# Row sums of the adaLN projection: a fixed place behind TensorE's order, a load per short step

## The chip, the core and the metric

The kernel runs on one NeuronCore of a Trainium2 chip. The metric is the time of one execution on the device in microseconds (us). Before the change, three runs gave 1697.73, 1699.33 and 1700.04 us, a median of 1699.33 us. An execution under the profiler took 1700.17 us, and its trace spans 1698.4 us.

The engines are TensorE (PE; PEld is its weight load), VectorE (DVE), ScalarE (ACT), GpSimd (POOL) and SyncE (SP), which here only issues DMA transfers, one after the other in one queue.

## What is computed

Two layers of a backbone block on 256 context tokens and 256 latent tokens of width 2048. Cut to what matters:

```python
def _layer(x, ctx, c, c_ctx, ...):
    shift, scale, gate = jnp.split(jax.nn.silu(c) @ w_ada + b_ada, 3, axis=-1)
    shift_c, scale_c, gate_c = jnp.split(jax.nn.silu(c_ctx) @ w_ada + b_ada, 3, axis=-1)
    h = _rms_norm(x, norm_w) * (1.0 + scale[:, None]) + shift[:, None]
    hc = _rms_norm(ctx, norm_w) * (1.0 + scale_c) + shift_c
    p = jnp.split(h @ w_in, offsets, axis=-1)       # and pc from hc
    ...                                             # four head groups: attention, LRU, DeltaNet, latent attention
    x = x + gate[:, None] * (jnp.concatenate([y_a, y_b, y_c, y_d], axis=-1) @ w_out)
    ...                                             # the same for ctx in the first layer
```

`w_ada` is 2048 x 6144 for each layer, and it is multiplied by two vectors only (the conditioning of the latent and of the context tokens). That product is what the change is about.

## The kernel before

**Projections.** Activations lie feature by token, 512 tokens wide. Each weight is split into a high and a low part (`hi`, `lo`), and a 128 x 128 block costs three matmuls. Weights come in units of 128 x 512: a load `raw` on SP's queue (3 buffers), `hi` by ScalarE, `lo = raw - hi` by VectorE (3 buffers each), then 12 matmuls into a `gm` buffer. `lo` is VectorE's part of every unit, so a late VectorE makes TensorE wait after at most the units that are already split. The last stage of each layer, the output projection, reads such units from `w_out` with `yhi` and `ylo` on the other side, and VectorE adds each result to the residual `xo`.

**adaLN by row sums.** Chunks 0 to 7 of layer 0 are computed on TensorE at the start (`ada_pe`). All others, 8 to 11 of layer 0, 0 to 7 of layer 1 (both during layer 0), and 8 to 11 of layer 1 (during layer 1), go through `ada_bg`: a chunk is 16 transfers of 128 x 512 from a transposed `w_ada` into `araw`, which has 2 buffers. For each, VectorE runs a SCALAR_TENSOR_TENSOR that multiplies by the conditioning vector `crow` and sums the rows into a column of `acc` (`aacc`). With two vectors it runs twice: the first writes its product to `junk`, the last over `araw` itself. The latent-only chunks of layer 1 need it once. That makes 192 loads with two row sums and 64 with one, 448 row sums. After a chunk, `ada_sum` folds `acc` by four small matmuls and adds the bias. A load can go out when the last row sum on its buffer is done.

**What sets the order.** Tasks are Python generators that a model clock (`Flow`) interleaves: each issued matmul moves the clock, and a task that yields a number sleeps so long. TensorE's instructions are pinned in the order in which they are issued (`in_order`); the weight loads are pinned among themselves (`load`, "load order"). All others are placed by a list scheduler with priorities, which simulates the engines and gives each a fixed order; on the chip an engine works through its own order and waits where an operand isn't there. `self.behind(i, name, why)` adds an edge that only the order sees: `i` may stand no earlier than `name`. It makes no wait on the chip.

In `ada_bg` before, each step issues a load and, at once, its row sums, at a lowered priority (`high_priority(-100)`); then it sleeps `self.pace` (2.8 in layer 0's projections, 4.0 in layer 1's, 2.0 in the output projections), and longer while the model of VectorE is over 1.0 us behind. Only each eighth load has an edge to the last weight load. The scheduler so puts the row sums where its own simulation has the transfer landed and VectorE free. `Flow` wakes tasks between groups of three matmuls, so steps come out in multiples of a group.

Of the kernel before, what the change touches and what calls it, by code (L numbers as in the profile page):

```python
# [191 lines left out]
class Block:  # L192
# [300 lines left out]
    def ada_bg(self, items):  # L493


        if not hasattr(self, "crow"):
            self.ada_rows()
        for l, ch in items:
            nv = 2 if l == 0 or ch < 8 else 1
            acc = self.st([128, nv, 16], "aacc")  # L500
            for j in range(16):
                raw = self.st([128, 512], "araw")
                i = self.nc.sync.dma_start(out=raw, in_=self.io["w_ada"][12 * l + ch - 8, j])
                if j % 8 == 0:
                    self.behind(i.ins, self.last_load, "load order")
                with self.tc.high_priority(-100):
                    for v in range(nv):
                        self.dve.scalar_tensor_tensor(
                            out=raw if v == nv - 1 else self.junk, in0=raw, scalar=1.0, in1=self.crow[:, v, :],
                            op0=ALU.mult, op1=ALU.mult, accum_out=acc[:, v, j:j + 1])  # L510
                yield self.pace
                while self.dve.behind() > self.LIM:
                    yield self.dve.behind() - self.LIM + 0.1
            self.flow.spawn(self.ada_sum(l, ch, acc), self.dve.behind() + self.rest)

    def ada_sum(self, l, ch, acc):
        p = self.pt([128, 4, acc.shape[1]])
# [966 lines left out]
    def layer(self, l):  # L1484
        nc, flow = self.nc, self.flow
        self.l = l
        self.qt = [0, 1, 2, 3] if l < LAYERS - 1 else [2, 3]
        self.t0 = 0 if l < LAYERS - 1 else TC
        self.yd = self.tc.dram_tile([12, 128, T], F32, name=f"yd{l}")
        self.hs, self.y, self.cq, self.cv = [], {}, {}, {}  # L1490
        self.vq = self.one([128, 4, 4], "vq")
        flow.done = {e for e in flow.done if e.startswith("ada")}
        flow.spawn(self.start0() if l == 0 else self.start1())
        pss = yield from (self.gemm_pairs if l == 0 else self.gemm_multi)(self.FIRST[l])
        if l == 0:
            self.pace, self.rest = 2.8, 14.0
            flow.spawn(self.ada_bg([(0, ch) for ch in range(8, 12)] + [(1, e) for e in range(8)]))
        else:
            self.pace, self.rest = 4.0, 14.0
            flow.spawn(self.ada_bg([(1, ch) for ch in range(8, 12)]))  # L1500
        flow.spawn(self.krab(pss[0]))
        if l == 0:
            flow.spawn(self.ak_tile(0, pss[5]))
        flow.spawn(self.c_keys(pss[1:5]))
        flow.spawn(self.c_scan())
        flow.spawn(self.d_split())
        flow.spawn(self.attend(self.a_chains()))
        flow.spawn(self.attend(self.d_chains()))
        todo = {"ak": self.ak_tile, "av": self.av_tile, "aq": self.aq_tile, "cq": self.cq_tile, "cv": self.cv_tile,
                "dkv": self.dkv_tile, "dq": self.dq_tile, "bx": self.bx_tile, "zb": self.zb_tile}  # L1510
        for name in self.ORDER[l]:
            if name in self.AFTER and (l == 0 or name != "dkv0"):
                yield self.AFTER[name]
            g, i = name[:-1], int(name[-1])
            if g == "up":
                yield from self.d_up(i)
                continue
            ps = yield from self.gemm(self.t0 if g in ("cq", "dq", "aq") or g[0] == "z" else 0)
            flow.spawn(todo[g](i, ps) if g in todo else self.z_tile(g[1], i, ps))
        yield "d3"  # L1520
        self.pace, self.rest = 2.0, 8.0
        if l == LAYERS - 1:
            self.rawtag, self.nraw = "r2", 5
        yield from self.out_proj(l)
# [137 lines left out]
```

## Time and profile before

| | before |
|---|---|
| median of three runs | 1699.33 us |
| the profiled execution | 1700.17 us, span 1698.4 us |
| TensorE busy | 1612.3 us (95%) |
| VectorE busy | 1210.3 us (71%) |
| ScalarE, GpSimd busy | 723.4 us (43%), 266.8 us (16%) |
| granted TensorE clock, mean | 0.986 |

Busy shares are means over stages that differ. TensorE's idle time is 86.1 us of the span. The row sums are the two SCALAR_TENSOR_TENSOR groups on `crow`; the numbers behind the bar in a group's row are its busy time, the mean of one in ns, and the time in which the engine stood idle before it, with what ended most of that wait. A wait of an engine in its own order also holds all that stands behind the waiting instruction.

### The profile page before, as it was taken

The page shows a single profiled execution, that of the slowest core. Times are in us where ns is not written, and L with a number is a line of the kernel's source. Part 1 is how long each engine was busy: PE and PEld are TensorE (multiplying, and loading weights), DVE is VectorE, ACT ScalarE, POOL GpSimd, SP SyncE. Part 2 cuts the span into 40 slices and gives each one's busy share as a digit, 9 for nine tenths or more (in the row PEclk, how much of TensorE's full clock was granted, in tenths as well). Part 3 has the DMA queues.
Part 4 walks back from the last instruction along what each step waited for, and adds up shares of the span by engine and source line. Part 5 has one row for each costly group of instructions (what it writes and reads, how often), then busy time and mean ns, then how long its engine had stood idle before and what let it go on. Part 6 is the DMA issues. An engine that isn't in the chain of part 4 may idle for free.

```text
span 1698.4 us, 27629 instructions
## 1 busy us (share of the span) xinstructions
PE 1612.3 (95%) x9888; PEld 1310.2 (77%) x9888; DVE 1210.3 (71%) x2852; ACT 723.4 (43%) x1365; POOL 266.8 (16%) x351
## 2 busy tenths in 40 slices
PE   3999999899999999999999998999899999999999
PEld 2666777678888877667877776778788989677899
DVE  4336877698888768787977758665766777565854
ACT  4224342243333344476522235445442324656843
POOL 0000327513032000000011100031842012100000
PEclk8999999999999999999999999999999999999999
DMA  8995435533523645435677645444554524433575
GB/s 311 333 345 178 143 109 147 149 117 112 159 79 95 204 144 159 134 114 172 198 226 228 209 137 155 139 132 121 169 176 129 174 88 141 118 100 105 180 231 155
DMA packets 145657, 276.61 MB, mean 163 GB/s; under 512 B 16620, under 2 KB 25712, under 8 KB 145520
## 3 DMA queue, kind: packets, MB, share of 16 engines
q1 hardware_dynamic: 143328, 269.81, 51.4%
q0 software_dynamic: 1328, 4.33, 1.1%
q8 instruction: 78, 1.28, 0.3%
q10 hardware_dynamic: 864, 0.71, 0.1%
q14 instruction: 59, 0.48, 0.1%
HBM read 261.81 MB, written 13.11 MB: 162 GB/s over the span
## 4 chain that ended last, share of the span: by engine, by line
PE 67%; DMA 12%; DVE 8%; POOL 6%; issue 6%; ACT 1%; SPq 0%; ACTq 0%; DVEq 0%; POOLq 0%
PE gm L231 42%; PE px L231 22%; DMA araw<-w_ada 9%; POOL Xs L184 3%; PE px L236 3%; POOL ct L184 2%; DVE lo L184 2%; DVE junk L184 1%; DMA ls<-C 1%; DVE araw L184 1%; DMA xk<-xT 1%; ACT hi L184 1%; DMA raw<-w_first 1%; DMA Ls<-ls 1%; DVE xo L184 0%
## 5 line engine op out<-in xcount | busy, mean ns | idle before, releaser
L231 PE MATMUL gm<-hhi,hi 128*128 128x512 f32 (+1 forms) x1296 | 497.3, 384 | 2.9 <-ACT hi L184 2.6
L184 ACT ACTIVATE hi<-raw 128x512 fp32r<-128x512 f32 (+1 forms) x454 | 282.2, 626 | 495.2 <-PE gm L231 334.8
L184 DVE TENSOR_TENSOR lo<-raw,hi 128x512 fp32r<-128x512 f32 (+1 forms) x454 | 325.6, 719 | 219.7 <-ACT hi L184 210.4
L231 PE MATMUL gm<-hhi,lo 128*128 128x512 f32 (+1 forms) x1296 | 463.6, 358 | 5.9 <-DVE lo L184 5.8
L231 PE MATMUL gm<-hlo,hi 128*128 128x512 f32 (+1 forms) x1296 | 461.1, 356 | 0.0
L231 PEld LDWEIGHTS gm<-hhi,hi 128*128 128x128 f32 x1296 | 246.3, 190 | 56.1 <-issue 24.5
L231 PEld LDWEIGHTS gm<-hhi,lo 128*128 128x128 f32 x1296 | 245.6, 190 | 44.9 <-DVE lo L184 8.2
L231 PEld LDWEIGHTS gm<-hlo,hi 128*128 128x128 f32 x1296 | 246.8, 190 | 32.7 <-issue 5.3
L184 DVE SCALAR_TENSOR_TENSOR araw<-araw,crow 128x512 f32<-128x512 f32 x256 | 185.1, 725 | 22.4 <-DMA araw<-w_ada 19.3
L184 DVE SCALAR_TENSOR_TENSOR junk<-araw,crow 128x512 bf16<-128x512 f32 x192 | 138.1, 719 | 48.9 <-DMA araw<-w_ada 48.3
L231 PE MATMUL gm<-yhi,lo 128*128 128x512 f32 (+1 forms) x416 | 141.8, 341 | 6.0 <-DVE lo L184 5.8
L231 PE MATMUL gm<-yhi,hi 128*128 128x512 f32 (+1 forms) x416 | 140.4, 337 | 0.0
L231 PE MATMUL gm<-ylo,hi 128*128 128x512 f32 (+1 forms) x416 | 140.0, 336 | 0.0
L231 PEld LDWEIGHTS gm<-yhi,lo 128*128 128x128 f32 x416 | 78.9, 190 | 20.8 <-DVE lo L184 13.0
L231 PEld LDWEIGHTS gm<-ylo,hi 128*128 128x128 f32 x416 | 79.0, 190 | 8.3
L231 PEld LDWEIGHTS gm<-yhi,hi 128*128 128x128 f32 x416 | 79.0, 190 | 7.5
L231 PE MATMUL px<-hhi,hi 128*128 128x512 f32 x176 | 75.0, 426 | 8.7 <-ACT hhi L184 7.7
L231 PE MATMUL px<-hlo,hi 128*128 128x512 f32 x176 | 71.9, 408 | 0.2 <-DVE hlo L184 0.2
L231 PE MATMUL px<-hhi,lo 128*128 128x512 f32 x176 | 71.1, 404 | 0.0
L231 PE MATMUL gm<-araw,csil 128*32 128x128 f32 x1024 | 38.5, 290 | 29.2 <-DMA araw<-w_ada 28.7
L184 DVE TENSOR_TENSOR lo<-r,hi 128x512 fp32r<-128x512 f32 x62 | 42.9, 692 | 32.7 <-ACT hi L184 30.8
L184 POOL TENSOR_TENSOR sqa<-sqa,sqx 128x512 f32<-128x512 f32 x12 | 17.9, 1494 | 278.1 <-ACT sqx L184 278.1
(326 smaller groups left out, 2505.3 us busy)
## 6 DMA issues: line engine op xcount, KB each, us to landing
raw<-w_in SPq DMA_DIRECT2D x344, 256.0 KB, 2.7
araw<-w_ada SPq DMA_DIRECT2D x256, 256.0 KB, 2.9
araw<-w_ada SPq DMA_DIRECT2D x64, 512.0 KB, 5.6
raw<-w_out SPq DMA_DIRECT2D x66, 256.0 KB, 2.8
r<-w_out SPq DMA_DIRECT2D x62, 256.0 KB, 3.3
raw<-w_first SPq DMA_DIRECT2D x24, 256.0 KB, 6.6
xk<-xT SPq DMA_DIRECT2D x16, 256.0 KB, 5.2
xo<-xT SPq DMA_DIRECT2D x16, 256.0 KB, 3.9
```

Of the source, the lines that this page charges most:

```text
L184: return getattr(self.eng, name)(*a, **kw)
L231: self.in_order(self.nc.tensor.matmul(out, lhsT=lhsT, rhs=rhs, start=start, stop=stop), us or max(n, 128) * passes / 2400.0)
L236: self.in_order(self.nc.tensor.transpose(out, in_, self.c["ident"][b:b + n, b:b + n]), 0.107)
```

## The change

A step now issues the load of row-sum item n, sleeps half a pace, issues the row sums of item n-1, and sleeps the other half. The row sums so are issued one and a half steps behind their load. Every load has an edge to the last weight load and one to the last issued matmul, and each row sum has an edge to the last matmul issued. `ada_sum` is started directly behind the last row sums of a chunk. The pace in layer 0's projections goes from 2.8 to 2.2; 4.0 and 2.0 stay. The number of instructions of each kind on each engine is unchanged.

```diff
-            acc = self.st([128, nv, 16], "aacc")
-            for j in range(16):
+        todo, raws, acc = [(l, ch, j) for l, ch in items for j in range(16)], [], None
+        for n in range(len(todo) + 1):
+            if n < len(todo):
+                l, ch, j = todo[n]
                 raw = self.st([128, 512], "araw")
                 i = self.nc.sync.dma_start(out=raw, in_=self.io["w_ada"][12 * l + ch - 8, j])
-                if j % 8 == 0:
-                    self.behind(i.ins, self.last_load, "load order")
+                self.behind(i.ins, self.last_load, "load order")
+                self.behind(i.ins, self.last_pe, "paced")
+                raws.append(raw)
+            yield 0.5 * self.pace
+            if n:
+                l, ch, j = todo[n - 1]
...
+                while self.dve.behind() > self.LIM:
+                    yield self.dve.behind() - self.LIM + 0.1
+                raw = raws.pop(0)
                 with self.tc.high_priority(-100):
                     for v in range(nv):
-                        self.dve.scalar_tensor_tensor(
+                        i = self.dve.scalar_tensor_tensor(
...
+                        self.behind(i.ins, self.last_pe, "paced")
+                if j == 15:
+                    self.flow.spawn(self.ada_sum(l, ch, acc), self.dve.behind() + self.rest)
+            yield 0.5 * self.pace
...
-            self.pace, self.rest = 2.8, 14.0
+            self.pace, self.rest = 2.2, 14.0
```

VectorE in layer 0's output projection. Before, where `lo_8471` and the next two `lo` stand (numbers tell buffers apart; `araw_8531` and `araw_8562` are two loads):

```order
L184 TENSOR_TENSOR lo_8471<-raw_8468,hi_8470 128x512
L184 SCALAR_TENSOR_TENSOR junk_1487,aacc_8530<-araw_8531,crow_1485 128x512
L184 TENSOR_TENSOR lo_8493<-raw_8490,hi_8492 128x512
L184 SCALAR_TENSOR_TENSOR araw_8531,aacc_8530<-araw_8531,crow_1485 128x512
L184 SCALAR_TENSOR_TENSOR junk_1487,aacc_8530<-araw_8562,crow_1485 128x512
L184 SCALAR_TENSOR_TENSOR araw_8562,aacc_8530<-araw_8562,crow_1485 128x512
L184 TENSOR_TENSOR lo_8515<-raw_8512,hi_8514 128x512
L184 SCALAR_TENSOR_TENSOR junk_1487,aacc_8530<-araw_8584,crow_1485 128x512
```

The same place of the projection now (`lo_8531` and the two after it; `araw_8495`, `araw_8526` and `araw_8548` are three loads):

```order
L184 TENSOR_TENSOR lo_8531<-raw_8528,hi_8530 128x512
L184 SCALAR_TENSOR_TENSOR junk_1487,aacc_8267<-araw_8495,crow_1485 128x512
L184 SCALAR_TENSOR_TENSOR araw_8495,aacc_8267<-araw_8495,crow_1485 128x512
L184 TENSOR_TENSOR lo_8553<-raw_8550,hi_8552 128x512
L184 SCALAR_TENSOR_TENSOR junk_1487,aacc_8267<-araw_8526,crow_1485 128x512
L184 SCALAR_TENSOR_TENSOR araw_8526,aacc_8267<-araw_8526,crow_1485 128x512
L184 TENSOR_TENSOR lo_8575<-raw_8572,hi_8574 128x512
L184 SCALAR_TENSOR_TENSOR junk_1487,aacc_8267<-araw_8548,crow_1485 128x512
```

The two row sums of a load now stand together, one pair behind each `lo`; before, a `lo` stood between them in one unit and two pairs followed each other in another.

SP's queue at that place, before:

```order
L503 DMA araw_8531<-w_ada 128x512
L503 DMA araw_8562<-w_ada 128x512
L265 DMA raw_8544<-w_out 128x512
L1544 DMA xo_9138<-xT 128x512
L645 DMA xk_9593<-x1d_8068 128x512
L265 DMA raw_8566<-w_out 128x512
L503 DMA araw_8584<-w_ada 128x512
L503 DMA araw_8606<-w_ada 128x512
```

And now:

```order
L503 DMA araw_8526<-w_ada 128x512
L265 DMA raw_8603<-w_out 128x512
L503 DMA araw_8548<-w_ada 128x512
L1554 DMA xo_9173<-xT 128x512
L265 DMA raw_8625<-w_out 128x512
L655 DMA xk_9593<-x1d_8129 128x512
L503 DMA araw_8570<-w_ada 128x512
L265 DMA raw_8647<-w_out 128x512
```

Loads of `araw` went out in pairs with a weight load behind them; now one stands between two weight loads.

VectorE in layer 1, at an attention head (`mx` and `P` belong to its softmax), before:

```order
L184 TENSOR_TENSOR lo_11437<-raw_11434,hi_11436 128x512
L184 SCALAR_TENSOR_TENSOR ya1_11443<-zt_11444,gm_11322 128x256
L184 TENSOR_REDUCE mx_11449<-px_11447 128x1
L184 SCALAR_TENSOR_TENSOR araw_11556,aacc_11417<-araw_11556,crow_1485 128x512
L184 TENSOR_TENSOR lo_11471<-raw_11468,hi_11470 128x512
L184 SCALAR_TENSOR_TENSOR mx_11449<-mx_11449,a_rs_10337 128x1
L184 SCALAR_TENSOR_TENSOR araw_11626,aacc_11417<-araw_11626,crow_1485 128x512
L184 RECIPROCAL mx_11449<-mx_11449 128x1
L184 TENSOR_SCALAR P_11452<-P_11452,mx_11449 128x512
L184 TENSOR_TENSOR lo_11505<-raw_11502,hi_11504 128x512
```

And now:

```order
L184 TENSOR_TENSOR lo_11423<-raw_11420,hi_11422 128x512
L184 SCALAR_TENSOR_TENSOR ya1_11429<-zt_11430,gm_11312 128x256
L184 TENSOR_REDUCE mx_11437<-px_11435 128x1
L184 SCALAR_TENSOR_TENSOR mx_11437<-mx_11437,a_rs_10333 128x1
L184 SCALAR_TENSOR_TENSOR araw_11332,aacc_10274<-araw_11332,crow_1485 128x512
L184 TENSOR_TENSOR lo_11459<-raw_11456,hi_11458 128x512
L184 RECIPROCAL mx_11437<-mx_11437 128x1
L184 TENSOR_SCALAR P_11440<-P_11440,mx_11437 128x512
L184 TENSOR_TENSOR lo_11491<-raw_11488,hi_11490 128x512
```

Row sums stood between two `lo` each time; now one stands where two stood, and its load went out well before the weight loads of these units.

## Rows read from the trace of the kernel before

**Rows 1.** The page: span, and busy time of the engines.
```profile
span 1698.4 us, 27629 instructions
PE 1612.3 (95%) x9888; PEld 1310.2 (77%) x9888; DVE 1210.3 (71%) x2852; ACT 723.4 (43%) x1365; POOL 266.8 (16%) x351
```

**Rows 2.** The page's groups of row sums: busy, mean ns, idle before, releaser.
```profile
L184 DVE SCALAR_TENSOR_TENSOR araw<-araw,crow 128x512 f32<-128x512 f32 x256 | 185.1, 725 | 22.4 <-DMA araw<-w_ada 19.3
L184 DVE SCALAR_TENSOR_TENSOR junk<-araw,crow 128x512 bf16<-128x512 f32 x192 | 138.1, 719 | 48.9 <-DMA araw<-w_ada 48.3
```

**Rows 3.** Waits of TensorE: total us, times, longest.
```profile
PE gm L231 <- DVE lo L184: 11.6, 15, 2.7
```

**Rows 4.** Busy by stretch: length, engines, clock, DMA share, GB/s.
```profile
255.00:849.00 594.00, 578.48 (x3027) 458.83 (x3026) 475.88 (x1173) 254.16 (x473) 106.84 (x132) 0.99 0.48 142
789.00:849.00 60.00, 60.00 (x265) 48.04 (x264) 54.19 (x115) 38.76 (x59) 0.00 (x0) 1.00 0.68 204
886.00:986.00 100.00, 94.42 (x410) 72.56 (x408) 78.68 (x187) 25.18 (x43) 13.22 (x9) 1.00 0.71 216
```

**Rows 5.** Chain of waits from 870 to 1000: start, us, what.
```profile
886.34 4.01 DMA araw<-w_ada
...
891.68 0.62 DVE araw L184 x2
...
892.32 3.59 DMA araw<-w_ada
...
898.65 3.17 DMA araw<-w_ada
```

**Rows 6.** The same stretches for instructions on gm, then on px.
```profile
886.00:986.00 100.00, 94.21 (x394) 72.25 (x392) 7.49 (x16) 0.00 (x0) 1.00 0.71 216
...
886.00:986.00 100.00, 0.50 (x16) 0.31 (x16) 0.53 (x4) 0.00 (x0) 1.00 0.71 216
```

**Rows 7.** Chain of waits, 535 to 564: matmuls in a row.
```profile
535.50 27.25 PE gm L231 x120
```

**Rows 8.** DMA issues from 860 to 1000; then of the whole span.
```profile
araw<-w_ada SPq DMA_DIRECT2D x39, 256.0 KB, 3.6
...
araw<-w_ada SPq DMA_DIRECT2D x256, 256.0 KB, 2.9
```

**Rows 9.** Timeline of VectorE: row sums that waited, idle time in brackets.
```profile
229.54 0.69 DVE L184 SCALAR_TENSOR_TENSOR junk<-araw,crow 128x512 bf16<-128x512 f32 x1 [1.96 <-DMA araw<-w_ada]
...
326.51 0.69 DVE L184 SCALAR_TENSOR_TENSOR junk<-araw,crow 128x512 bf16<-128x512 f32 x1 [3.37 <-DMA araw<-w_ada]
...
1204.66 1.01 DVE L184 SCALAR_TENSOR_TENSOR araw<-araw,crow 128x512 f32<-128x512 f32 x1 [1.43 <-DMA araw<-w_ada]
...
1240.69 0.69 DVE L184 SCALAR_TENSOR_TENSOR araw<-araw,crow 128x512 f32<-128x512 f32 x1 [0.99 <-DMA araw<-w_ada]
...
1245.13 0.69 DVE L184 SCALAR_TENSOR_TENSOR araw<-araw,crow 128x512 f32<-128x512 f32 x1 [0.86 <-DMA araw<-w_ada]
```

**Rows 10.** Timeline of TensorE: matmuls that waited.
```profile
239.15 0.42 PE L236 MATMUL px<-cst,P 128*128 128x128 f32 x2 [2.53 <-DVE P L184]
...
327.95 0.63 PE L231 MATMUL gm<-hhi,lo 128*128 128x512 f32 x1 [2.73 <-DVE lo L184]
...
1206.71 0.38 PE L231 MATMUL gm<-hhi,lo 128*128 128x256 f32 x1 [2.07 <-DVE lo L184]
...
1248.31 0.66 PE L236 MATMUL px<-cst,P 128*128 128x128 f32 x4 [3.19 <-DVE P L184]
```

**Rows 11.** Timelines of GpSimd and ScalarE around a chain on GpSimd.
```profile
288.13 0.94 POOL L184 TENSOR_TENSOR ct<-Ls,Xs 128x238 f32<-128x238 f32 x1
...
293.89 0.62 POOL L184 TENSOR_TENSOR ct<-Ls,Xs 128x238 f32<-128x238 f32 x1
...
314.17 0.21 ACT L184 ACTIVATE gw<-rowp 128x8 f32<-128x8 f32 x1 [8.14 <-POOL Xs L184]
```

**Rows 12.** Waits of SP's queue, 860 to 1000: total us, times, longest.
```profile
SPq L503 <- DVE araw L184: 24.2, 28, 1.9
```

More of the change, by code (lines that the diff above doesn't have):

```diff
@@ L497, in ada_bg @@
             self.ada_rows()
-        for l, ch in items:
-            nv = 2 if l == 0 or ch < 8 else 1
-            acc = self.st([128, nv, 16], "aacc")
-            for j in range(16):
+        todo, raws, acc = [(l, ch, j) for l, ch in items for j in range(16)], [], None
+        for n in range(len(todo) + 1):
+            if n < len(todo):
+                l, ch, j = todo[n]
                 raw = self.st([128, 512], "araw")
                 i = self.nc.sync.dma_start(out=raw, in_=self.io["w_ada"][12 * l + ch - 8, j])
-                if j % 8 == 0:
-                    self.behind(i.ins, self.last_load, "load order")
+                self.behind(i.ins, self.last_load, "load order")
[4 more added lines that the diff above has]
+                l, ch, j = todo[n - 1]
+                nv = 2 if l == 0 or ch < 8 else 1
+                if j == 0:
+                    acc = self.st([128, nv, 16], "aacc")
+                while self.dve.behind() > self.LIM:
+                    yield self.dve.behind() - self.LIM + 0.1
+                raw = raws.pop(0)
                 with self.tc.high_priority(-100):
                     for v in range(nv):
-                        self.dve.scalar_tensor_tensor(
+                        i = self.dve.scalar_tensor_tensor(
                             out=raw if v == nv - 1 else self.junk, in0=raw, scalar=1.0, in1=self.crow[:, v, :],
                             op0=ALU.mult, op1=ALU.mult, accum_out=acc[:, v, j:j + 1])
[L511 to L514, printed above, removed]
+                        self.behind(i.ins, self.last_pe, "paced")
+                if j == 15:
+                    self.flow.spawn(self.ada_sum(l, ch, acc), self.dve.behind() + self.rest)
+            yield 0.5 * self.pace
     def ada_sum(self, l, ch, acc):
```

## The prediction

> **What bounds the kernel now.** I read the page's busy times first. TensorE works 1612.3 us of the 1698.4 us span [rows 1]; the change adds no matmul and takes none away, so all it can give is a part of the 86.1 us in which TensorE stands idle. Then the groups of row sums: VectorE stood 48.3 + 19.3 = 67.6 us before row sums whose transfer had not landed [rows 2]. VectorE is not the bound, so those 67.6 us are no gain by themselves. What they cost is read one view further: in its waits TensorE lost 11.6 us to `lo`, in 15 pieces [rows 3].
>
> Where does `lo` come late? In 886 to 986 us, layer 0's output projection, TensorE is busy 94.42 of 100 us [rows 4]. The busy figure hides a part, because each restart lengthens a matmul. So I count: 394 matmuls on `gm` [rows 6] at the undisturbed pace of 27.25 / 120 = 0.227 us [rows 7] need 89.5 us, the 16 small ones 0.5 us [rows 6]. That makes 90.0 us of work in 100 us: **10 us lost** there. The chain of waits shows by what. It runs through `araw` loads, not through TensorE: a load at 886.34 takes 4.01 us, row sums follow, and the next load of that buffer goes out at 892.32, the one after at 898.65 [rows 5]. So one turn of a buffer takes 5.98 and 6.33 us. With two buffers, two loads go through per turn, one for each unit of weights; two units are 24 matmuls, 24 x 0.227 = 5.45 us. The turn is slower than TensorE, so the row sums set the pace, and `lo` stands behind them in VectorE's order.
>
> The other places are single ones: TensorE stood 2.73 us at 327.95 behind a `lo` that stood behind a row sum idle for 3.37 us; 2.07 us at 1206.71, behind one idle for 1.43 us; 3.19 us at 1248.31 for `P`, before which two row sums waited 0.99 and 0.86 us; 2.53 us at 239.15 for `P`, with 1.96 us before [rows 9, 10].
>
> **The change, part by part.** The row sums stay 448, at about 0.70 us each (means of 0.725 and 0.719, which overlap a little with what follows) [rows 2]. What moves is where they stand.
>
> *Distance from load to row sum.* Counted in the programs, in the order in which each lists the instructions of all engines, 11 to 13 matmuls stand in most cases between an `araw` load and its first row sum before: 12 x 0.227 = 2.7 us. A load takes 2.9 us in the median, and 3.6 us in 860 to 1000 [rows 8]; so the typical row sum waits a little. Now it is 16 to 20 matmuls in layer 0, 18 x 0.227 = 4.1 us, above both medians, and 35 or more in layer 1, 8 us. I expect the 67.6 us of waits to fall to 10 to 20 us.
>
> *Output projection.* The turn of a buffer is now landing plus its own two row sums, 3.6 + 1.4 = 5.0 us, since no `lo` stands between the pair any more, plus about 0.1 us to issue. That is under the 5.45 us of two units, by 0.35 us only. Bounds: 0, if late loads eat that margin, and the whole 10 us. The medians favour the upper part, the margin is thin: I take **6 us**.
>
> *327.95.* One load far over the median; a distance of 4.1 us instead of 2.7 takes most of the 3.37 us of idle time, and two units of split weights the rest. Bounds 0 and 2.73; I take **2.7**.
>
> *Layer 1.* The waits before 1206.71 and 1248.31 go: bounds 0 and 2.07 + 0.99 + 0.86 = 3.9; I take **3.0**, since `P` has other inputs. What is late next at 1248.31 is the softmax's own chain, so the rest of its 3.19 stays.
>
> *239.15.* Bounds 0 and 1.96; I take **1.0**, because the row sums still stand before `P` there. Together 6 + 2.7 + 3.0 + 1.0 = 12.7 us.
>
> *Shorter steps.* With 2.2 instead of 2.8 the model issues one load per weight unit, where it was fewer. In the programs' orders the row sums between the 50th and the 200th `lo` (255 to 849 us before) grow from 249 to 282; the first 50 units lose 12, the last of layer 0 lose 21, and the last row sum of layer 0 comes ten units earlier. 33 x 0.70 = 23.1 us more VectorE in a stretch where it is busy 475.88 of 594 us, 80% [rows 4]; it becomes 84%. Bounds: 0, and 23.1 us if each of them delays what TensorE waits for. The nearest row is 789 to 849, where VectorE is at 54.19 of 60 us and TensorE at 60.00 of 60 [rows 4]: at 90% nothing got through. I take a tenth, **2.3 us**.
>
> *The chain on GpSimd.* While GpSimd solves its triangular system, 263 to 314 us, VectorE's share decides how fast: the same `ct` step took 0.94 us beside a busy VectorE and 0.62 us beside an idle one. ScalarE waits 8.14 us for that chain's end before `gw`, with `hi` queued behind, and `gw` keeps its place [rows 11]. The stretch gets 24 row sums instead of 21: 3 x 0.70 = 2.1 us of VectorE time, a third of which (0.32 of 0.94) GpSimd loses: **0.7 us**, between 0 and 2.1. This is where a rule speaks against the change: the Trainium skill, "SBUF — State Buffer", section "SBUF: two separate sides", says that a VectorE instruction with two inputs in SBUF and a GpSimd instruction that reads SBUF take a shared port in turn, the one blocking the other for a whole instruction. A row sum has two such inputs; by that rule GpSimd would lose all 2.1 us and the sum would be worse by 1.4. The two `ct` steps agree in direction; a block for a whole instruction each time isn't what their 0.32 us shows.
>
> *SP's queue.* Every load now stands behind the last weight load, and weight loads stand behind it. It waits on SP until its buffer is free, as it does now (24.2 us in 28 waits, 860 to 1000, 0.86 us each [rows 12]). Behind it stand weight loads that TensorE needs three units later, 3 x 2.72 = 8.2 us, less 3.6 us to land as an `araw` load does [rows 8] and two passes of some 0.7 us for `hi` and `lo`: about 3.2 us of cover for a wait of 1.9 us at most. I cost it at nothing; if the waits passed 3.2 us, TensorE would stop for the rest of each.
>
> *The folding matmuls* stand in TensorE's order 43 to 141 matmuls behind the last row sum of a chunk, before 70 to 413: at least 43 x 0.227 = 9.8 us of cover. Nothing, unless VectorE falls that far behind.
>
> Sum: 12.7 - 2.3 - 0.7 = **9.7 us less**. The profiled execution took 1700.17 us, 1.8 over its span; it becomes 1690.5, and from the median of the runs, 0.84 us lower, **1689.6 us**.
>
> **Rivals.**
> *A. Two buffers still bind.* No buffer is added; the order alone changes. If late loads use up the 0.35 us of margin, the projection gives 0 of its 6 us: 1699.3 - 3.7 = 1695.6. For it: the second load of the chain took 3.59, the first 4.01, and with 4.01 the turn is 5.5, just the 5.45 needed. Against it: the average need only be under. The Trainium skill, "Perfetto Trace Analysis", Optimization Strategy, says that a gap which repeats on the engine that should be full can mean too few buffers; the repeated turns in the chain agree, and by that rule alone the time would be this 1695.6.
> *B. The next waiter takes the place.* TensorE's order is dense with attention and DeltaNet chains whose own inputs are late; of the places above only the 2.07 and 2.73 name `lo`. If three quarters of the gain is so lost: 12.7 / 4 - 3.0 = 0.2, so 1699. Against it: in the output projection nothing but `lo` is waited for.
> *C. VectorE too full in the middle, slower.* The 33 row sums more in 255 to 849 stand in front of `mx`, `P` and `lo` in an order that can't be left. It decides from the point at which over half of their 23.1 us reaches TensorE (12.7 - 0.7 = 12 gained elsewhere); at three quarters, 17.3 us, the time is 1699.3 + 5.3 = 1704.6. For it: TensorE is idle 15.5 us there already, with VectorE at 80% in the mean, more in places [rows 4]. Against it: 60.00 of 60 at 90%.
> That the edges do nothing is excluded, since the orders show the pairs and distances moved.
>
> **How the numbers follow.** The forecast, 1682 to 1694, 0.46; more than that, where the projection gives its 10 us and the costs are nothing, 0.08; A 0.15, B 0.14, C 0.17. Of A some two thirds lie over 0.2% (3.4 us, about what measurement can tell from no change) below. Faster: 0.46 + 0.08 + 0.10 = 0.64; same: 0.05 + 0.14 = 0.19; slower: 0.17. The low end takes all bounds of gain: 10 + 2.7 + 3.9 + 2.0 = 18.6, so 1680.7, and some 3 us for the small waits that I left out: 1678. The high end reaches B and most of C: 1703. The forecast's own range is 1682 to 1694.
>
> **What would show it.** Right: idle time before row sums at a third of 67.6 or less; the chain in the output projection runs through TensorE; 100 us of it hold over 410 matmuls on `gm`; TensorE's waits for `lo` fall from 11.6 to about 4 us. Wrong: loads still on the chain with turns over 5.45 us (A); the same idle total of TensorE with other names (B); TensorE idle well over 15.5 us in 255 to 849 (C); a longer wait before `gw` than 8.14 us, for the price of GpSimd.

## The result and the profile after

The changed kernel takes 1679.25 us in the median of four runs (1678.93 to 1682.83), the kernel before 1699.68 us in the median of its four (1697.73 to 1703.21). The ratio is **0.9882, 95% interval [0.9861, 0.9903]**: 20.4 us less, where 9.7 were forecast. That is below the forecast's own range of 1682 to 1694 us, in the upper case of gain to which the prediction gave a chance of 0.08, and inside its outer bounds of 1678 to 1703. The profiled execution took 1678.93 us. Its page has for span and busy times:

```profile
span 1677.2 us, 27630 instructions
PE 1602.2 (96%) x9888; PEld 1310.4 (78%) x9888; DVE 1215.2 (72%) x2852; ACT 724.2 (43%) x1365; POOL 267.2 (16%) x351
```

TensorE's idle time fell from 86.1 us [rows 1] to 1677.2 - 1602.2 = 75.0 us. That is 11.1 us, half of the 21.2 us that the span lost. The busy time fell too, by 10.1 us with the same 9888 matmuls, since a matmul between waits counts as busy for longer: 94.21 us for 394 of them in the output projection before [rows 6], 0.239 us each, at a granted clock of 1.00, against 0.227 at full pace. Where the clock falls behind a wait it is longer still (the rows at 239 us below).

The two groups of row sums (busy, mean ns, idle before, releaser):

```profile
L184 DVE SCALAR_TENSOR_TENSOR araw<-araw,crow 128x512 f32<-128x512 f32 x256 | 186.5, 728 | 3.7
L184 DVE SCALAR_TENSOR_TENSOR junk<-araw,crow 128x512 bf16<-128x512 f32 x192 | 135.4, 705 | 22.4 <-DMA araw<-w_ada 21.9
```

67.6 us of waiting for `araw` [rows 2] became 21.9. TensorE's waits (total us, times, longest):

```profile
PE gm L231 <- ACT hi L184: 8.5, 1, 8.5
...
PE gm L231 <- DVE lo L184: 3.5, 2, 3.3
PE px L236 <- POOL FG L184: 2.8, 2, 1.5
```

`lo` costs 3.5 us instead of 11.6 [rows 3]. A single wait of 8.5 us for `hi` stands out; at the same matmul it was 2.55 us before:

```profile
314.95 0.79 PE L231 MATMUL gm<-hhi,hi 128*128 128x512 f32 x1 [2.55 <-ACT hi L184]
```

By stretch (length, busy time of PE, PEld, DVE, ACT, POOL, then granted clock, DMA share, GB/s), with the stretches shifted to the same places in the work:

```profile
249.00:842.00 593.00, 578.62 (x3042) 459.90 (x3041) 498.47 (x1247) 255.72 (x477) 106.31 (x132) 0.99 0.50 150
782.00:842.00 60.00, 60.00 (x265) 48.04 (x264) 56.96 (x128) 39.41 (x60) 0.00 (x0) 1.00 0.68 215
868.00:968.00 100.00, 100.00 (x455) 82.37 (x454) 73.01 (x165) 27.83 (x46) 13.35 (x9) 1.00 0.70 219
```

The middle carries 22.6 us more VectorE work than before (475.88 [rows 4]) and no cost to TensorE can be seen (it idles 593.00 - 578.62 = 14.4 us there, 15.5 before): in 782 to 842 it is at 60.00 of 60 beside a VectorE at 56.96. In the output projection it stands still no more. The same 100 us for instructions on `gm`:

```profile
868.00:968.00 100.00, 99.78 (x439) 82.06 (x438) 8.62 (x18) 0.00 (x0) 1.00 0.70 219
```

439 matmuls instead of 394 [rows 6], 0.227 us each: the full pace. The transfers did not get faster (issue to landing, 842 to 982), and SP still waits for the buffers there (total us, times, longest):

```profile
araw<-w_ada SPq DMA_DIRECT2D x31, 256.0 KB, 3.6
```

```profile
SPq L503 <- DVE araw L184: 28.6, 27, 2.6
```

3.6 us as before [rows 8], 28.6 us of waiting on SP against 24.2 [rows 12]; the longest, 2.6 us, stays under the 3.2 us of cover. Row sums still wait for transfers there. VectorE's waits, 860 to 1000 before, then 842 to 982 after:

```profile
DVE junk L184 <- DMA araw<-w_ada: 21.8, 23, 2.1
...
DVE junk L184 <- DMA araw<-w_ada: 8.2, 10, 1.6
```

Nor did the turn of a buffer fall under the 5.45 us of two weight units. With two buffers, every second load is on the same one. SP's issues after:

```profile
882.31 0.33 SPq L503 DMA_DIRECT2D araw<-w_ada  x1
...
884.26 0.33 SPq L503 DMA_DIRECT2D araw<-w_ada  x1
...
888.37 0.33 SPq L503 DMA_DIRECT2D araw<-w_ada  x1
...
890.32 0.33 SPq L503 DMA_DIRECT2D araw<-w_ada  x1
```

Two turns of 6.06 us; over the 31 loads of this stretch the median is 5.77 us, against 6.09 over those of 862 to 980 before.

To see where the time came from I count matmuls: both programs issue 9888, and the start of the k-th is read from the records, one trace for each kernel. Times between such marks are in us. The first 1600 took 203.0 and 203.1 us.

| matmuls | what lies there | before | after | difference |
|---|---|---|---|---|
| 1600 to 2600 | first heads, solve on GpSimd | 198.8 | 191.2 | -7.6 |
| 2600 to 5000 | middle of layer 0 | 469.7 | 468.1 | -1.6 |
| 5000 to 5700 | output projection of layer 0 | 174.0 | 164.4 | -9.6 |
| 5700 to 9887 | layer 1 | 649.2 | 646.4 | -2.8 |

Timeline of TensorE after, matmuls that waited (in brackets):

```profile
312.67 0.79 PE L231 MATMUL gm<-hhi,hi 128*128 128x512 f32 x1 [8.49 <-ACT hi L184]
...
330.36 1.09 PE L236 MATMUL px<-cst,FG 128*128 128x128 f32 x8 [1.34 <-POOL FG L184]
...
1218.59 0.39 PE L231 MATMUL gm<-hhi,lo 128*128 128x256 f32 x1 [3.29 <-DVE lo L184]
```

The four waits of [rows 10] have no counterpart. The largest now is that of 8.49 us. Its cause is one instruction of ScalarE, with `hi` behind it; `gw`, an exponential for layer 1, takes the buffer of `ct`, one of the two tiles that the chain on GpSimd works on:

```profile
311.89 0.21 ACT L184 ACTIVATE gw<-rowp 128x8 f32<-128x8 f32 x1 [14.63 <-POOL Xs L184]
```

It waited 8.14 us before [rows 11]. The end of the GpSimd chain moved only from 314.1 to 311.9 us; ScalarE came to it earlier. (`FG` at 330.36 holds blocks of that chain's result, which TensorE transposes.) The new wait for `lo` at 1218.59 stands behind another chain: the `mx` of an attention head, with `lo` behind it in VectorE's order, waits for `a_rs` of GpSimd.

```profile
1217.21 0.32 DVE L184 SCALAR_TENSOR_TENSOR mx<-mx,a_rs 128x1 f32<-128x1 f32 x1 [5.30 <-POOL a_rs L184]
```

This head waited for `a_rs` before too, in the same order of `mx` and `lo`, but no wait of TensorE followed:

```profile
1235.89 0.28 DVE L184 SCALAR_TENSOR_TENSOR mx<-mx,a_rs 128x1 f32<-128x1 f32 x1 [2.47 <-POOL a_rs L184]
```

### The profile page after: what moved, and what is told of

Read it like the earlier page. It is cut to its first block, busy times and chain, and to the rows that moved or that the text cites. A ratio compares the mean times of both kernels' runs of the same rounds, so it can differ in the third digit from the quotient of the medians.

```text
span 1677.2 us, 27630 instructions
## 1 busy us (share of the span) xinstructions
PE 1602.2 (96%) x9888; PEld 1310.4 (78%) x9888; DVE 1215.2 (72%) x2852; ACT 724.2 (43%) x1365; POOL 267.2 (16%) x351
## 3 DMA queue, kind: packets, MB, share of 16 engines
q1 hardware_dynamic: 143328, 269.81, 51.5%
## 5 line engine op out<-in xcount | busy, mean ns | idle before, releaser
L184 DVE SCALAR_TENSOR_TENSOR junk<-araw,crow 128x512 bf16<-128x512 f32 x192 | 135.4, 705 | 22.4 <-DMA araw<-w_ada 21.9
L184 ACT ACTIVATE hi<-r 128x512 fp32r<-128x512 f32 x62 | 39.2, 632 | 50.2 <-PE gm L231 39.6
```

The costliest lines, as they stand in the source:

```text
L184: return getattr(self.eng, name)(*a, **kw)
```

## The experiments

Each was timed in three rounds beside the kernel before on the same chip. A table of all stands at the end of this section; the rows that decide stand with each.

**Shorter steps alone.** The kernel before, with one number changed:

```diff
-            self.pace, self.rest = 2.8, 14.0
+            self.pace, self.rest = 2.2, 14.0
```

> The kernel before with the pace of layer 0's projections at 2.2 instead of 2.8, nothing else. Row sums between the 50th and the 200th lo: 290 instead of 249, in the output projection 46 instead of 87; the distance from a load to its first row sum stays at a median of 12 to 14 matmuls. Distance theory (the gain of 20 us comes from row sums that stand far enough behind their load): the turns in the output projection end earlier, since fewer loads are left there, so 3 to 6 us less than before, 1694 to 1697 us, and VectorE still idles 50 to 70 us before row sums. Pace theory (the gain comes from having the row sums out of the output projection): most of the 20 us, 1680 to 1685 us.

Measured: ratio 1.0016 [0.9998, 1.0035]. Waits before row sums are 16.6 + 59.6 = 76.2 us, more than before. In the middle (2600 to 5000) the kernel loses 6.4 us, in the output projection it gains 2.5 us, as fewer row sums are left for it. Neither expectation came true; the distance theory had 3 to 6 us less. So shorter steps without the distance are worth nothing in sum. A slower middle, as in rival C, exists: it comes when row sums are packed closer and still stand right behind their loads, not from a full VectorE, for the changed kernel packs them as close there.

**Distance and load edges without a place for the row sums.** The changed kernel, less one line:

```diff
-                        self.behind(i.ins, self.last_pe, "paced")   # on the row sums
```

> The changed kernel without the edge from a row sum to the last matmul; loads keep theirs, and pace, lag of issue and counts stay (282 and 64 row sums in the two stages). The scheduler puts the row sums back to a median of 11 to 13 matmuls behind their load. Distance theory: the gain is mostly gone, 1692 to 1700 us, with 50 us or more of idle time before row sums. Pace theory: the gain stays, 1679 to 1684 us. If the gain came from how the rest of the order fell, anything between, without a link to that idle time.

Measured: 0.9944 [0.9922, 0.9965], about half of the gain, where the distance theory had it mostly gone. The early gain stays (193.0 us from 1600 to 2600), the output projection gains 1.8 us only, and waits before row sums are back at 15.5 + 55.0 us. There the window on `gm`, 880 to 980, reads:

```profile
880.00:980.00 100.00, 95.30 (x405) 74.83 (x404) 7.50 (x16) 0.00 (x0) 1.00 0.62 195
```

405 matmuls, not 439. In the output projection the edge on the row sums is needed. In 1600 to 2600 it is not, and there the gain came without shorter waits of the row sums. VectorE's waits in that stretch, before, changed, and here:

```profile
DVE junk L184 <- DMA araw<-w_ada: 8.2, 8, 3.4
...
DVE junk L184 <- DMA araw<-w_ada: 4.6, 4, 2.7
...
DVE junk L184 <- DMA araw<-w_ada: 11.9, 12, 2.5
```

**Edges on the loads taken back.** The other half of the same question:

```diff
-                self.behind(i.ins, self.last_load, "load order")
-                self.behind(i.ins, self.last_pe, "paced")
+                if j % 8 == 0:
+                    self.behind(i.ins, self.last_load, "load order")
```

> The changed kernel without the two edges of each load (every eighth load keeps the one to the last weight load, as before the change); row sums keep edges and lag, medians of 24 and 18 matmuls. Distance theory: the whole gain stays, 18 to 22 us less than before. If the early part came from the spread of the loads (the run without edges on the row sums kept 6 us of it), 10 to 14 us less than before.

Measured: 0.9867 [0.9839, 0.9896], within the interval of the changed kernel, 21.6 us of waits, 165.2 us for the output projection. The edges on the loads give nothing that can be seen; the issue a step and a half behind, with the edge on the row sums, does it.

**The changed kernel with the old density.** Half steps of 1.1 and 1.7 instead of 1.1 and 1.1 in layer 0's projections (the second is shown; the comment is mine):

```diff
-            yield 0.5 * self.pace
+            yield 1.7 if self.pace == 2.2 else 0.5 * self.pace   # the second half step
```

> The changed kernel with the two halves of a step in layer 0's projections at 1.1 and 1.7 instead of 1.1 and 1.1: about the density of before (240 row sums between the 50th and the 200th lo, 249 before), 113 left for the output projection, with edges and lag kept (medians of 25 and 18 matmuls). Distance theory: the projection still runs at TensorE's pace, and the end of layer 0 waits a little for the last row sums, 1680 to 1686 us. Pace theory: 1693 us or more, with the output projection slower than before.

Measured: 0.9901 [0.9874, 0.9928], which overlaps the changed kernel's interval, so on the whole it is not told apart. The trace does differ in the output projection: 167.6 us instead of 164.4, 414 matmuls on `gm` in 878 to 978, with VectorE at 80.30 us of 100 instead of 69.11 (877 to 977 of the changed kernel, the same place in the work). The middle takes 470.0 us, and 468.1 in the denser changed kernel. The density costs nothing that can be seen there.

**The change in one stage alone.** Distance and edges only in the output projections (pace 2.8 elsewhere, as before), and then only in layer 0's projections (pace 2.2 there). The edit is cut to what differs; the comments stand for the code left out:

```diff
+            if self.pace == 2.0:      # the second kernel: if self.pace == 2.2
+                ...                   # load, half a step, row sums of the item before, as changed
+                continue
+            load(n, False)            # as before
+            s = rows(False)
+            yield self.pace
```

> Lag and edges only in layer 0's output projection; in its projections (pace 2.8) and in layer 1 the row sums are issued as before the change. The distance from load to row sum is 18 matmuls in the median in the output projection and 13.5 and 18.5 elsewhere, as before; 92 row sums stand in the output projection (87 before, 66 in the changed kernel). Distance theory: the projection's 9.7 us come back, nothing else, 8 to 11 us less than before. If the gain of that stage came from fewer row sums in it: 0 to 2 us less than before.

> Lag and edges only in layer 0's projections (pace 2.2, 284 row sums there with a median of 23 matmuls behind their load); in the output projection and in layer 1 as before (medians of 12.5 and 18.5). Distance theory: the 9 us up to the output projection stay and of that projection's 9.7 us only what its fewer row sums bring (64 instead of 87, 2 to 3 us): 10 to 12 us less than before. If the early part of the gain is chance in the order, anything from 2 us.

Measured: 0.9958 [0.994, 0.9976] for the first, 0.993 [0.9903, 0.9957] for the second. The first leaves the early stretch nearly as it was (197.8 us) and gains 7.3 us in the output projection; the second has the whole early gain (191.4 us) and 2.4 us in the output projection, about what shorter steps alone gave there. The second came as expected (some 12 us less than before); the first gave 6 to 7 us where 8 to 11 were expected. The window of the first, 886 to 986, all instructions:

```profile
886.00:986.00 100.00, 98.25 (x440) 79.16 (x439) 86.38 (x207) 26.27 (x44) 14.22 (x9) 1.00 0.75 230
```

VectorE does more here than in the kernel before (86.38 against 78.68 us [rows 4]), and yet TensorE goes from 94.42 to 98.25 us. Distance works without less work. The rest to 100.00 goes with fewer row sums: of `araw` pairs, 33 stand in 842 to 982 of the changed kernel, 44 in 860 to 1000 of this one and 40 in 860 to 1000 before.

**`gw` held back.** After the result I took the 8.49 us wait at 312.67 for the next thing to gain. `gw` got an edge to the last matmul, so that ScalarE does `hi` first:

```diff
-        self.act(nea, row[:, 0:8], AF.Exp)
+        i = self.sca.activation(out=nea, in_=row[:, 0:8], func=AF.Exp, scale=1.0, bias=0.0)
+        self.behind(i.ins, self.last_pe, "paced")
```

> The changed kernel, and the exponential of layer 1's a_log (gw<-rowp, ScalarE) gets an edge to the last matmul issued, so that it stands in layer 1 and not in layer 0 behind GpSimd's chain. If that wait of ScalarE (14.63 us in the changed kernel) is what holds TensorE for 8.49 us at 304 us, with the clock at half for 10.2 us after it, both go: 9 to 14 us less than the changed kernel, 1665 to 1670 us. If GpSimd's chain is needed just behind by others (the DeltaNet scan), the wait moves there and the time is 1676 to 1680 us.

Measured: 0.9889 [0.9866, 0.9913], no gain. TensorE's wait for `hi` is gone, and the next reader of the same chain takes its place (waits of TensorE):

```profile
PE px L236 <- POOL FG L184: 17.7, 2, 15.4
```

The chain on GpSimd itself got longer. First instruction to last `Xs`, of before, after and this kernel (columns as above):

```profile
263.30:314.10 50.80, 46.78 (x225) 37.51 (x217) 38.32 (x85) 13.73 (x28) 46.17 (x65) 0.97 0.47 135
```

```profile
260.40:311.90 51.50, 43.78 (x213) 35.19 (x212) 37.84 (x83) 13.55 (x29) 46.86 (x65) 0.96 0.43 131
```

```profile
260.40:318.70 58.30, 57.60 (x283) 46.40 (x279) 54.74 (x122) 19.56 (x38) 53.66 (x65) 1.00 0.59 168
```

With TensorE running on, VectorE worked 54.74 - 37.84 = 16.9 us more beside the chain, and the chain took 6.8 us more for the same 65 instructions: 0.40 us for each us of VectorE. That the one causes the other is not shown, as no run changed VectorE's work alone.

**FG later in TensorE's order.** In that kernel, the transposes on `FG` are now issued later. In the traces the first stands 91 matmuls later (76 by the expectation):

```diff
-        yield 11.0
+        yield 27.0        # at the end of the solve
```

> The changed kernel with the edge on ScalarE's gw as in the run before, and the model's time for the way back from GpSimd's chain 27.0 instead of 11.0, so that TensorE's first transpose of FG stands 76 matmuls later in its order (some 17 us). If what is left at 304 to 333 us is a wait of TensorE for GpSimd's chain that stands too early in its order, the wait of 15.39 us with 17.1 us at half clock goes: 10 to 18 us less than the changed kernel. If all that follows the chain comes later by as much and is waited for there, no gain: within 4 us of the changed kernel.

Measured: 0.9845 [0.9812, 0.9879]. The wait for FG is 2.40 us, and 1600 to 2600 take 184.2 us. Less came out than was expected, for layer 1 lost 4.8 us against the changed kernel (651.2 against 646.4). By the whole time it is not told apart from the changed kernel, whose interval it overlaps; the stretch shows the gain.

**FG later, `gw` free again.** Only the last edit, on the changed kernel.

> The changed kernel with one number changed: the matmuls on FG stand 76 matmuls later in TensorE's order; `gw` is free again to stand ahead of `hi` in ScalarE's order. Theory (both ends of the GpSimd chain have to leave the way, `gw` on ScalarE and FG on TensorE): ScalarE again waits over 10 us before `gw`, TensorE waits some 8 us for `hi` behind it, no gain over the changed kernel: 1679 to 1683, ratio about 0.989. Rival (FG on TensorE is all that counts): 1675, ratio 0.9845, and no wait of TensorE over 3 us between 290 and 340 us.

Measured: 0.9876 [0.9853, 0.99], no gain over the changed kernel, as the theory had it: 191.4 us from 1600 to 2600. TensorE waits 8.54 us for `hi` again, behind (timeline of ScalarE):

```profile
312.95 0.21 ACT L184 ACTIVATE gw<-rowp 128x8 f32<-128x8 f32 x1 [14.64 <-POOL Xs L184]
```

Both readers have to move; each alone leaves the other in the way.

**Both later, load edges taken back.** The two edits and the one above on the loads.

> The version with `gw` and FG both later, with the edges on the row-sum loads taken back (only each eighth load behind the last weight load, none behind the last matmul). Theory (the edges on the loads give nothing, what counts is the place of the row sums): like that version, ratio 0.9845, 1673 to 1677. Rival (the two gains add, since without load edges the time was 0.9867 against 0.9882): 1672, ratio 0.982.

Measured: 0.9825 [0.9806, 0.9843], which overlaps the version with the edges; whether the edges cost something is not settled. In this trace the chain of waits reaches back through the output projection (start, us, what), which it doesn't in the changed kernel's:

```profile
849.15 38.76 PE gm L231 x171
887.91 0.18 PE px L231 x8
888.09 43.78 PE gm L231 x192
```

No load stands on it any more, a sign that the changed kernel's own trace can't give. Layer 1 took 654.6 us here. There the same late FG pushes the DeltaNet chain against its own next steps (timeline of TensorE):

```profile
1345.10 1.01 PE L236 MATMUL px<-cst,R 128*4 128x128 f32 x4 [4.85 <-DVE R L184]
```

**FG later in layer 0 alone.** 

```diff
-        yield 27.0
+        yield 11.0 if self.l else 27.0
```

> The version with `gw` and FG both later and free row-sum loads, with FG later in layer 0 alone; in layer 1 it stands in TensorE's order where the changed kernel has it. Theory (the later FG cost 10 us in layer 1, where the 200 matmuls from the 7600th took 42.0 us against 31.5, since the DeltaNet chain behind FG was pushed against its own next steps; TensorE waited 4.85 us for R there): the two gains add, 1663 to 1668, ratio about 0.977. Rival (those matmuls are work that comes elsewhere, so what layer 1 loses there it loses anywhere): like the version before it, 1672 to 1676, ratio 0.9825.

Measured: 1669.21 us in the median, ratio **0.9815 [0.9794, 0.9835]**, the fastest median of the study, and clear of the changed kernel's interval, though not of the version before it. Layer 1 takes 643.3 us, 11.3 less than in the version before it. The 200 matmuls from the 7600th on, there and here:

```profile
1320.50:1362.50 42.00, 33.31 (x202) 28.31 (x201) 30.17 (x56) 8.24 (x15) 8.37 (x7) 0.88 0.31 88
```

```profile
1326.20:1357.60 31.40, 31.24 (x202) 27.44 (x201) 22.12 (x44) 9.16 (x17) 2.24 (x2) 1.00 0.39 115
```

The stretch came out as the theory had it, the time did not: it is above the 1663 to 1668 given. In these two traces the first 1600 matmuls and the output projection took 204.7 - 199.6 + 166.5 - 164.8 = 6.8 us longer than in the version before. The edit does not touch these places, so this looks like the spread between executions (the first 1600 matmuls take 199.6 to 204.7 us over all the traces), but it isn't settled. By the whole time alone the two are not told apart.

All together (idle: waits before row sums; the next four: us between matmuls; `gm`: matmuls in 100 us of the output projection):

| kernel | ratio | idle | 1600-2600 | 2600-5000 | 5000-5700 | 5700-9887 | `gm` |
|---|---|---|---|---|---|---|---|
| before | 1 | 67.6 | 198.8 | 469.7 | 174.0 | 649.2 | 394 |
| changed | 0.9882 | 21.9 | 191.2 | 468.1 | 164.4 | 646.4 | 439 |
| shorter steps alone | 1.0016 | 76.2 | 200.5 | 476.1 | 171.5 | 649.1 | 416 |
| no edge on row sums | 0.9944 | 70.5 | 193.0 | 470.0 | 172.2 | 649.0 | 405 |
| no edges on loads | 0.9867 | 21.6 | 191.2 | 468.4 | 165.2 | 646.6 | 439 |
| old density | 0.9901 | 34.1 | 191.2 | 470.0 | 167.6 | 645.4 | 414 |
| output projections only | 0.9958 | 59.6 | 197.8 | 470.8 | 166.7 | 651.2 | 424 |
| layer 0's projections only | 0.993 | 49.3 | 191.4 | 468.0 | 171.6 | 651.2 | 411 |
| `gw` later | 0.9889 | 17.7 | 196.0 | 468.1 | 164.5 | 645.4 | 439 |
| `gw` and FG later | 0.9845 | 17.3 | 184.2 | 467.5 | 164.4 | 651.2 | 440 |
| FG later | 0.9876 | 21.9 | 191.4 | 467.5 | 164.6 | 652.2 | 439 |
| both, no load edges | 0.9825 | 16.4 | 181.7 | 469.0 | 164.8 | 654.6 | 440 |
| both, FG in layer 0 only | 0.9815 | 17.0 | 181.4 | 467.5 | 166.5 | 643.3 | 434 |

## Why the prediction was right, and where its sizes were off

The direction was right, and the prediction named the distance from load to row sum as what gives it. The size was half of what was measured, and in the output projection the sum that was to justify the gain did not come true.

**Waits of row sums**, forecast 10 to 20 us of 67.6: 21.9. Right in kind, a little over. The edge on the row sums carries it (70.5 us without).

**Output projection**, forecast 6 of 10 us: 9.6. The prediction let the thin margin of a buffer's turn, 0.35 us, cost 4 us. The margin did not come: the turn was to be 5.1 us and is 5.77 us in the median, over the 5.45 us from which it was to hold TensorE up. Yet TensorE waited for nothing in 868 to 968, with 28.6 us of waiting on SP and 8.2 us before row sums. So a turn over 5.45 us is not by itself what costs; from these rows, what costs is a row sum that waits so long that the `lo` behind it comes late. And it missed a second source: it booked the shorter steps as a cost in the middle alone, while each row sum done there is one less here. The two kernels with one half each show it: distance alone gave 7.3 us, density alone 2.5 (2.4 in the kernel with layer 0's projections only).

**327.95 and 239.15**, forecast 2.7 + 1.0: the stretch gave 7.6. Both waits went, and so did one of 2.31 us for `P` at 289 and three for ScalarE's `csq` (3.2 us, 359 to 402) that the prediction had not listed. Of idle time the stretch lost only 3.3 us net (13.3 to 10.0 us, summed over waits over 0.15 us), for the wait for `hi` grew from 2.55 to 8.49 us: the gain ran into the GpSimd chain, of which more below. What the sum lacked is the price of the clock behind a wait. Timeline of TensorE before, around the wait at 239.15, then the window behind it:

```profile
236.23 0.39 PE L231 MATMUL gm<-hhi,lo 128*128 128x512 f32 x1
...
239.31 0.68 PE L231 MATMUL gm<-hhi,hi 128*128 128x512 f32 x1
239.79 0.63 PE L231 MATMUL gm<-hlo,hi 128*128 128x512 f32 x1
240.22 0.63 PE L231 MATMUL gm<-hhi,lo 128*128 128x512 f32 x1
```

```profile
239.20:242.80 3.60, 3.60 (x16) 3.31 (x17) 3.49 (x12) 1.11 (x4) 0.00 (x0) 0.53 0.47 116
```

After 2.53 us of standing still the matmuls start 0.43 us apart instead of 0.23, and the granted clock is 0.53 for 3.6 us, about the lower of the two levels (1.2 of 2.4 GHz). TensorE is "busy" in all of it. An estimate from these rows: 3.6 x (1 - 0.53) = 1.7 us beside the 2.53, two thirds more. Four such stretches lie between 200 and 400 us before, at 239.4, 290.6, 314.5 and 328.2; after there is one, which begins inside the wait of 8.49 us. Length, busy time of TensorE, granted clock, DMA share, GB/s, before and then after:

```profile
239.42:242.83 3.41, 3.41 (x16) 0.50 0.50 123
290.62:294.03 3.41, 3.41 (x14) 0.50 0.09 23
314.51:317.92 3.41, 2.97 (x7) 0.50 0.66 226
328.17:331.58 3.41, 3.41 (x9) 0.50 0.64 168
```

```profile
308.23:318.47 10.24, 5.80 (x14) 0.50 0.43 134
```

TensorE worked 13.2 us at half the clock before and 5.8 after; half of the difference, 3.7 us, and the 3.3 us of idle time make 7.0 of the 7.6 us, by this estimate. That the issue a step and a half behind, not the density, is the cause is shown: the kernels that do so in these projections have the gain (191.2 to 193.0 us, at either density; only where `gw` alone stands later does the wait for FG take most of it), the two that don't haven't (197.8, 200.5). That it works here through shorter waits of the row sums, as the prediction had it, is not shown: without the edge on them they waited 11.9 us in this stretch, more than the 8.2 us of before, and 5.8 us of the gain stayed.

**Layer 1**, forecast 3.0: 2.8, a size met by luck, for it is not made up as the sum had it. Small as it is, it stands clear in the table: the kernels that leave layer 1's row sums as they were take 649.1 to 651.2 us there, those with distance and edges in it 643.3 to 646.6, as long as FG isn't later in it. Both waits went whole, 2.07 + 3.19 us, also the part of the second that the prediction kept. Against that stand the new ones for `lo`, 3.29 us at 1218.59 behind `mx`, and for FG, 1.50 us at 1239.53. This is rival B in small.

**33 more row sums in the middle**, forecast a cost of 2.3: the middle became 1.6 us shorter, too little to tell from nothing. The bound of 0 was right; the tenth that I took can't be seen. Where the density comes without the distance, it costs 6.4 us.

**The chain on GpSimd**, forecast 0.7: 50.8 became 51.5 us, the same size by luck: VectorE was busy 37.84 us beside it, not more than the 38.32 before, so the reason given isn't borne out here. The sign for being wrong, a wait before `gw` over 8.14 us, came (14.63) and was badly chosen: the wait grew because ScalarE came sooner. What the prediction missed is that this chain is a floor. All that was won ahead of 312 us beyond the chain's own earlier start, from 263.3 to 260.4, turned into waiting for it. The kernels with `gw` and FG later show what lay there: 7.0 us (191.2 to 184.2), 9.8 in the last one.

On how GpSimd and VectorE block each other, the prediction set aside the rule of the Trainium skill, "SBUF — State Buffer", section "SBUF: two separate sides" (one of the two has the port for a whole instruction, the other waits), since `ct` lost only 0.32 us. That was a misreading: by that rule, who comes while the other is at work waits for the rest of it alone, so 0.32 us beside a row sum of 0.69 is no counter-example. The last section has rows of this trace that agree with the rule.

**SP's queue and the folding matmuls**, forecast nothing: behind the start no wait of TensorE names a transfer, and SP's longest wait in the output projection was 2.6 us.

**Rivals.** A (two buffers still bind) fell with 439 matmuls at full pace and two buffers, although its condition, turns over 5.45 us, holds. B (the next waiter takes the place) is true of two places, 312 and 1218 us, and false in the sum. C did not come in the changed kernel; a slower middle came in the one with shorter steps alone, through row sums that wait for their loads.

## What to carry to other kernels

A consumer in a fixed order that waits for a transfer holds up all that stands behind it: place it by the landing time, counted in instructions of the engine that sets the pace, and tie it to that order, so that the scheduler can't move it back. Before booking a gain, look for the next fixed point behind it, here a chain on a slow engine, and for all its readers, since moving one reader alone gains nothing. A wait of the bound engine costs more than its length when the clock falls with it (some 1.7 us beside 2.53 at 239 us), so count instructions per stretch, not idle time.

## What the runs showed of the hardware that was not expected

GpSimd holds up VectorE, it seems, and not only the reverse. In the output projection of the changed kernel seven `lo` and one row sum, of about 0.69 us elsewhere, take 1.42 to 1.77 us, and each begins inside one of the first eight of GpSimd's eleven `sqa` additions from 864 us on. VectorE, then GpSimd:

```profile
898.74 1.76 DVE L184 TENSOR_TENSOR lo<-raw,hi 128x512 fp32r<-128x512 f32 x1
...
901.76 0.69 DVE L184 TENSOR_TENSOR lo<-raw,hi 128x512 fp32r<-128x512 f32 x1
...
910.16 1.77 DVE L184 TENSOR_TENSOR lo<-raw,hi 128x512 fp32r<-128x512 f32 x1
```

```profile
898.33 1.62 POOL L184 TENSOR_TENSOR sqa<-sqa,sqx 128x512 f32<-128x512 f32 x1 [10.55 <-ACT sqx L184]
...
909.66 1.73 POOL L184 TENSOR_TENSOR sqa<-sqa,sqx 128x512 f32<-128x512 f32 x1 [9.71 <-ACT sqx L184]
```

The `lo` at 898.74 ends at 900.50, 0.55 us after the end of `sqa` at 899.95, a little less than an undisturbed `lo` takes. In each of the last three `sqa` a `lo` begins late, with 0.48 us of it left, and takes 1.03 us, 0.55 more than that rest (VectorE, then GpSimd):

```profile
952.20 1.03 DVE L184 TENSOR_TENSOR lo<-raw,hi 128x512 fp32r<-128x512 f32 x1 [1.68 <-ACT hi L184]
```

```profile
951.39 1.29 POOL L184 TENSOR_TENSOR sqa<-sqa,sqx 128x512 f32<-128x512 f32 x1 [9.50 <-ACT sqx L184]
```

So the length follows the rest of GpSimd's instruction, as if `lo` waited it out and then did its work; no experiment took `sqa` away to show it. The trace of before has twelve such instructions in its output projection (1.33 to 1.78 us), so the change neither brought nor removed the effect. The Trainium skill, "SBUF — State Buffer", section "SBUF: two separate sides", says that a VectorE instruction with two inputs in SBUF is blocked by a GpSimd instruction that started first, for the whole of it; these rows agree.

The reverse would be the longer chain on GpSimd beside a busier VectorE, 0.40 us for each us, in the run on `gw` above.
